# Another order for an encoder layer: transposes no longer kept in runs, shared transfer rates and two-way waits between VectorE and GpSimd in the MLP

## The chip, the cores and the metric

The kernel runs on one core of a Trainium2 chip. The time is the device time of one execution in microseconds (us); it was 708.28 us in the median of three runs. The engines of a core are TensorE (PE, matrix products and transposes), VectorE (DVE), ScalarE (ACT), GpSimd (POOL) and SyncE (SP, which here only issues transfers). PEld is the loading of weights into PE. Each engine takes its instructions in the order in which the program lists them, and waits on semaphores for the others.

## The reference

One layer (SEQ 512, D_MODEL 1024, D_FF 2816): a combined input projection feeds three groups of attention heads (A differential, B with forget gates, C over chunks), then an output projection, a gated MLP with a causal convolution of width 3, and a gated embedding.

```python
def reference(x, p, ln_mix, w_in, ...):
    h = x
    for i in range(DEPTH):
        hn = rms_norm(h, ln_mix[i])
        z = hn @ w_in[i]
        (q1, q2, k1, k2, va, qf, kf, vf, fg, qc, kc, vc) = jnp.split(z, IN_SPLITS, axis=-1)
        ...
        o_a = diff_attention(q1, q2, k1, k2, va, lam, subln_gain[i], lam_init)
        o_b = forgetting_attention(qf, kf, vf, log_f)
        o_c = chunk_attention(qc, kc, vc, rel_bias[i])
        h = h + jnp.concatenate([o_a, o_b, o_c], axis=-1) @ w_out[i]
        h = h + conv_gated_mlp(rms_norm(h, ln_ffn[i]), w_up[i], conv_w[i], conv_b[i], w_down[i])
        gate = jax.nn.sigmoid(rms_norm(h, ln_ple[i]) @ w_ple_gate[i])
        h = h + (p[i] @ w_ple_proj[i]) * gate
    return h

def conv_gated_mlp(h, w_up, conv_w, conv_b, w_down):
    u = h @ w_up
    ...
    gate, val = jnp.split(c, 2, axis=-1)
    return (jax.nn.silu(gate) * val) @ w_down
```

## The kernel before

All large products are made three times in a reduced format: an operand is cast to a high part (`whi`, `Th`, made by ACT) and the remainder is a low part (`wlo`, `Tl`, a DVE subtraction), and PE adds high·high, high·low and low·high into one PSUM bank. So each block of weights, 128 by 768 numbers, costs a transfer into `wraw` (SP queue), a cast, a subtraction, and then PE's products. Scores are `s<-k,q`, probabilities are `e`, transposed by PE against `ident` into banks `t`, and multiplied with `V` into `o`. `z`, `s`, `t` and `o` are the PSUM banks (2, 2, 3 and 1 of them). The sums for the queries' and keys' norms end in POOL powers (`rs<-rs,nhalf`) and POOL scalings (`k<-k`, `q<-q`).

In the MLP some of the products are made from sums of weight blocks, by a scheme that saves products (`up_seven`, `down`). POOL forms the sums (`wraw<-wraw,wraw`), or a transfer on POOL's own queue adds one block onto another on its way in; names with `again` are tiles used a second time.

Nothing of this is issued when the Python code runs through it. Each instruction is recorded in a `Plan` with a price; there is one plan for attention (from the first products to the output projection), another for the MLP and the rest. `Plan.due` gives each PE instruction a due time, the sum of the PE work recorded before it plus a number for its group from the table `SHIFT`; other engines' instructions are due before their readers. `Plan.solve` then walks forward in time: of the instructions that are free on an engine it takes the one due first. `Plan.emit` issues them in that order, and the order on each engine is pinned. Because of that every recorded instruction has the line of the one helper that issues it: L357 before (in `Engine.now`), L391 after the change.

Four rules of `solve` and `emit` belong to the change:

- Transfers: one wire for both queues, served in turn, at a rate of 0.37 MB per us for SP and 0.105 for POOL, with 2.0 us ahead and 0.6 behind.
- Runs of transposes: when PE has just made a transpose, another one that is free is preferred to a matmul (and the other way round) if it is due no more than `STICK` = 2.0 us later; a matmul after a lone transpose is priced 0.08 us higher.
- PE prefers instructions whose inputs have been ready for `SURE` = 0.1 us.
- Waits without data ("port"): in the second plan (`late` is 0.1 there and 0 in the first) a POOL instruction of over 0.6 us that follows a DVE instruction with all its inputs in SBUF is made to wait for it. `Engine.behind` adds such a wait.

Of the kernel before, what the change touches and what calls it, by code (L numbers as in the profile page):

```python
# [41 lines left out]
for _i in range(3):  # L42
# [5 lines left out]
AHEAD = 2  # L48
# [75 lines left out]
class Plan:  # L124
# [5 lines left out]
    def __init__(self, clock, there=(), mem=None, fresh=0.0, late=0.0):  # L130
        self.group, self.loaded, self.fresh, self.late = "first", set(), fresh, late
        self.clock, self.there, self.ops, self.mem = clock, [(v.tensor.name, self.region(v), t) for v, t in there], [], mem or {}

    @staticmethod
    def region(v):
        size = 2 if v.dtype == BF16 else 4
        (row, pn), *rest = [tuple(x) for x in v.ap]
        if v.tensor.space == bass.MemoryType.DRAM and v.tensor.name not in STAND_INS:
# [45 lines left out]
    def price(self, op):  # L184
# [4 lines left out]
        op.move, op.turns = 0, op.name == "transpose"  # L189
# [29 lines left out]
    LONG, STICK = 0.6, 2.0  # L219
    HW, SW, AT_ONCE = 0.37e6, 0.105e6, 8  # L220
    SURE, AHEAD, MUCH, WAIT = 0.1, 1.0, 2.0, 0.6
# [3 lines left out]
    def due(self, shift):  # L225
# [5 lines left out]
        for op in reversed(self.ops):  # L231
            if op.eng.name != "pe":
                spent = op.busy + op.lag + 0.05 + (op.move / self.HW + 2.0 if op.move else 0.0)
                op.dl = min([q.dl for q in op.next], default=t) - spent

    def solve(self):
# [6 lines left out]
        wire, out, order = 0.0, {"sp": [], "pool": []}, []  # L243
        turns, alone = False, False
        held = {"dve": 0.0, "pool": 0.0}
        other = {"dve": "pool", "pool": "dve"}
        when = lambda q: max(q.at, held[other[q.eng.name]] + (self.late if q.eng.name == "pool" else 0.0)) if q.port else q.at
        rank = lambda q: (q.dl, q.pos)
        while True:
            best = None  # L250
            for e in self.ENGINES:
                if free[e]:
                    t = max(clock[e], min(when(q) for q in free[e]))
                    if best is None or t < best[0]:
                        best = t, e
            if best is None:
# [3 lines left out]
            if e == "pe":  # L260
                can = [q for q in can if q.at + self.SURE <= t] or can
            op = min(can, key=rank)
            if e == "pe" and op.turns != turns:
                same = [q for q in can if q.turns == turns and q.dl < op.dl + self.STICK]
                if same and (turns or sum(q.turns and q.dl < op.dl + self.STICK for q in can) < 2 or min(q.dl for q in same) < op.dl + self.STICK / 2):
                    op = min(same, key=rank)
# [12 lines left out]
            if e == "pe":  # L279
                busy += 0.08 * (alone and not op.turns)  # L280
                turns, alone = op.turns, op.turns and not turns
            if op.move:
                done = out[e]
                if len(done) >= self.AT_ONCE:
                    t0 = max(t0, done[-self.AT_ONCE])
                wire = max(t0 + 2.0, wire) + op.move / (self.HW if e == "sp" else self.SW)
                op.end = wire + 0.6
                done.append(op.end)
# [7 lines left out]
            for q in op.next:  # L296
                q.left -= 1
                q.at = max(q.at, op.start if e == "pe" and q.eng is op.eng else op.end + self.LEAD[q.eng.name])
                if not q.left:
                    free[q.eng.name].append(q)  # L300
# [4 lines left out]
    def emit(self):  # L305
# [3 lines left out]
        before = None  # L309
        for op in self.choose():  # L310
            op.ins = op.eng.now(op.name, [real(v) for v in op.a], {q: real(v) for q, v in op.k.items()})
            if op.port:
                if before and op.eng.name == "pool" and before.eng.name == "dve" and op.busy > self.LONG and self.late:
# [1744 lines left out]
```

## Time and profile before

| | us |
|---|---|
| runs | 709.49, 708.25, 708.28 (median 708.28) |
| profiled execution, its own time | 707.89 |
| its span (first to last instruction) | 706.0 |
| granted clock of TensorE in it, mean | 0.998 |

| engine | busy us | share of the span |
|---|---|---|
| PE | 690.3 | 98% |
| DVE | 552.5 | 78% |
| ACT | 408.7 | 58% |
| POOL | 300.6 | 43% |

The costliest groups of instructions, by line, engine, operation, names and tile, then count, busy us, mean ns of one, and the engine's idle time before them with what ended it:

```profile
L357 ACT CAST whi<-wraw 128x768 fp32r<-128x768 f32 (+2 forms) x140 | 106.1, 768 | 59.9 <-POOL wraw L357 11.4
L357 PE MATMUL z<-whi,Th 128*128 128x384 f32 (+2 forms) x356 | 123.4, 351 | 4.5 <-ACT whi L357 4.5
L357 DVE TENSOR_TENSOR wlo<-wraw,whi 128x768 fp32r<-128x768 f32 (+2 forms) x122 | 111.5, 930 | 15.4 <-ACT whi L357 13.6
L357 POOL TENSOR_TENSOR wraw<-wraw,wraw 128x256 f32<-128x256 f32 (+1 forms) x22 | 28.3, 1285 | 101.3 <-DVE wlo L357 53.6
```

The mean duration of a matmul is longer than its spacing, since the next one starts before the last one's end: 128x512 matmuls follow each other at 0.233 us, 384 columns at 0.174, 256 at 0.118, transposes at 0.109. Where the text speaks of a loss, it is the distance from start to start less this spacing. A DVE, ACT or POOL instruction that is idle on its own account says nothing; what counts is whether PE waits.

### The profile page before, as it was taken

The page shows a single profiled execution, that of the slowest core. Times are in us where ns is not written, and L with a number is a line of the kernel's source. Part 1 is how long each engine was busy: PE and PEld are TensorE (multiplying, and loading weights), DVE is VectorE, ACT ScalarE, POOL GpSimd, SP SyncE. Part 2 cuts the span into 40 slices and gives each one's busy share as a digit, 9 for nine tenths or more (in the row PEclk, how much of TensorE's full clock was granted, in tenths as well). Part 3 has the DMA queues.
Part 4 walks back from the last instruction along what each step waited for, and adds up shares of the span by engine and source line. Part 5 has one row for each costly group of instructions (what it writes and reads, how often), then busy time and mean ns, then how long its engine had stood idle before and what let it go on. Part 6 is the DMA issues. An engine that isn't in the chain of part 4 may idle for free.

```text
span 706.0 us, 12402 instructions
## 1 busy us (share of the span) xinstructions
PE 690.3 (98%) x4420; PEld 636.4 (90%) x4420; DVE 552.5 (78%) x1126; ACT 408.7 (58%) x781; POOL 300.6 (43%) x403
## 2 busy tenths in 40 slices
PE   7999999999999999999999999999999999999997
PEld 7999999898999888899998999889988888999886
DVE  7679878879788666789888887997877998878722
ACT  6657676565766575666666435665345674536711
POOL 3788677766665452223223334304432203245200
PEclk9999999999999999999999999999999999999999
DMA  9523444423112252584763278651488552204521
GB/s 321 201 83 111 125 117 128 118 60 109 45 61 76 75 124 83 200 244 105 214 159 113 68 186 207 163 162 33 139 211 209 183 168 82 91 32 155 163 85 46
DMA packets 41275, 92.72 MB, mean 131 GB/s; under 512 B 4694, under 2 KB 7510, under 8 KB 41212
## 3 DMA queue, kind: packets, MB, share of 16 engines
q1 hardware_dynamic: 34572, 78.24, 33.1%
q0 software_dynamic: 6352, 13.38, 10.8%
q8 instruction: 35, 0.57, 0.3%
q10 hardware_dynamic: 288, 0.30, 0.1%
q14 instruction: 28, 0.23, 0.1%
HBM read 83.63 MB, written 4.21 MB: 124 GB/s over the span
## 4 chain that ended last, share of the span: by engine, by line
PE 91%; DVE 3%; DMA 2%; ACT 2%; POOL 1%; issue 1%; ACTq 0%; POOLq 0%
PE z L357 46%; PE s L357 22%; PE t L357 16%; PE o L357 7%; DMA wraw<-in_w_up_dram 1%; DVE wlo L357 1%; POOL k L357 1%; POOL q L357 1%; ACT whi L357 1%; DMA zn<-in_w_in_dram 0%; DVE e L357 0%; DVE conv L357 0%; POOL rs L357 0%; ACT e L357 0%; DVE kl L357 0%
## 5 line engine op out<-in xcount | busy, mean ns | idle before, releaser
L357 ACT CAST whi<-wraw 128x768 fp32r<-128x768 f32 (+2 forms) x140 | 106.1, 768 | 59.9 <-POOL wraw L357 11.4
L357 PE MATMUL z<-whi,Th 128*128 128x384 f32 (+2 forms) x356 | 123.4, 351 | 4.5 <-ACT whi L357 4.5
L357 DVE TENSOR_TENSOR wlo<-wraw,whi 128x768 fp32r<-128x768 f32 (+2 forms) x122 | 111.5, 930 | 15.4 <-ACT whi L357 13.6
L357 PE MATMUL z<-wlo,Th 128*128 128x384 f32 (+2 forms) x356 | 123.0, 350 | 0.0
L357 PE MATMUL z<-whi,Tl 128*128 128x384 f32 (+2 forms) x356 | 121.8, 347 | 0.0
L357 PEld LDWEIGHTS z<-whi,Th 128*128 128x128 f32 x356 | 66.9, 189 | 8.0 <-ACT whi L357 4.5
L357 POOL TENSOR_TENSOR wraw<-wraw,wraw 128x256 f32<-128x256 f32 (+1 forms) x22 | 28.3, 1285 | 101.3 <-DVE wlo L357 53.6
L357 PEld LDWEIGHTS z<-wlo,Th 128*128 128x128 f32 x356 | 67.2, 189 | 4.0 <-DVE wlo L357 0.4
L357 PEld LDWEIGHTS z<-whi,Tl 128*128 128x128 f32 x356 | 67.0, 189 | 3.8
L357 ACT ACTIVATE e<-e,st 128x128 f32<-128x128 f32 (+3 forms) x80 | 44.7, 560 | 29.8 <-DVE st L357 29.4
L357 PE MATMUL z<-Th,whi 128*128 128x512 f32 (+1 forms) x156 | 53.2, 346 | 1.4 <-ACT whi L357 1.3
L357 PE MATMUL s<-Th,whi 128*128 128x512 f32 (+1 forms) x156 | 53.3, 345 | 0.6 <-ACT whi L357 0.6
L357 PE MATMUL s<-Th,wlo 128*128 128x512 f32 (+1 forms) x156 | 53.7, 345 | 0.0
L357 PE MATMUL s<-Tl,whi 128*128 128x512 f32 (+1 forms) x156 | 53.6, 345 | 0.0
L357 PE MATMUL z<-Tl,whi 128*128 128x512 f32 (+1 forms) x156 | 53.5, 344 | 0.0
L357 PE MATMUL z<-Th,wlo 128*128 128x512 f32 (+1 forms) x156 | 53.4, 344 | 0.0
L357 POOL TENSOR_TENSOR rs<-rs,nhalf 128x4 f32<-128x4 f32 x40 | 43.5, 1091 | 4.8 <-DVE rs L357 2.3
L357 DVE CUSTOM_DVE_ANT_0 e<-s,bias 128x128 f32<-128x128 f32 (+3 forms) x74 | 33.7, 469 | 12.4 <-PE s L357 7.2
L357 DVE TENSOR_TENSOR conv<-conv,conv 128x512 f32<-128x512 f32 (+1 forms) x31 | 21.0, 691 | 24.0 <-ACT conv L357 23.8
L357 POOL TENSOR_SCALAR e<-e,st 128x512 f32<-128x512 f32 (+3 forms) x48 | 27.2, 576 | 18.1 <-DVE st L357 16.8
L357 PEld LDWEIGHTS z<-Th,whi 128*128 128x128 f32 x156 | 29.1, 188 | 4.8 <-ACT whi L357 1.8
L357 PEld LDWEIGHTS s<-Th,whi 128*128 128x128 f32 x156 | 29.2, 188 | 3.8 <-ACT whi L357 0.8
(352 smaller groups left out, 2152.4 us busy)
## 6 DMA issues: line engine op xcount, KB each, us to landing
wraw<-in_w_up_dram SPq DMA_DIRECT2D x41, 384.0 KB, 4.3
wraw<-in_w_in_dram SPq DMA_DIRECT2D x28, 384.0 KB, 3.7
wraw<-in_w_down_dram SPq DMA_DIRECT2D x16, 384.0 KB, 3.6
whi_again<-in_w_up_dram SPq DMA_DIRECT2D x11, 384.0 KB, 4.5
wraw<-in_w_out_dram SPq DMA_DIRECT2D x16, 256.0 KB, 2.7
wlo_again<-in_w_up_dram SPq DMA_DIRECT2D x10, 384.0 KB, 4.3
wraw<-in_w_up_dram SPq DMA_DIRECT2D x15, 256.0 KB, 4.1
wlo<-wraw POOLq DMA_DIRECT2D x7, 384.0 KB, 4.2
```

What stands on the lines that cost most here:

```text
L357: ins = getattr(self.eng, op)(*a, **k)
```

## The change

The `SHIFT` table gets other numbers for all of its groups. The runs of transposes are no longer kept and the 0.08 us for a lone transpose go. `SURE` becomes an argument: 0.15 us in the first plan, and in the second the fifth argument, 0.1, that was `late`, is now `sure`. In the second plan each queue has its own transfers in flight, at rates that depend on whether the other queue moves data too; the first plan (`apart=True`) has both queues at their single rates, independent of each other. The waits without data are set both ways: an instruction of over 0.25 us of either engine waits for the other engine's last one if it is planned to start less than `NEAR` after that one's end; in the first plan none is set, as before. The last line of `region` tells the planner which parts of the output two stores touch.

```diff
@@ Plan.__init__ @@
-    def __init__(self, clock, there=(), mem=None, fresh=0.0, late=0.0):
+    def __init__(self, clock, there=(), mem=None, fresh=0.0, sure=0.15, apart=False):
+        self.sure, self.apart = sure, apart
+        if apart:
+            one = {"sp": 0.37e6, "pool": 0.105e6}
+            self.RATE, self.SENT, self.ARRIVED = {k: {e: one[e] for e in k} for k in self.RATE}, {"sp": 2.0, "pool": 2.0}, 0.6
+            self.HANDED = {"pool": 0.0, "dve": 0.0}
@@ SHIFT @@
-    "first": -11.4, "in1_0": -0.3, "in1_1": -25, "in1_2": -2.7, "A0a": -6.5, "in1_3": -12.1, "in2_0": -5.9,
...
@@ constants @@
-    LONG, STICK = 0.6, 2.0
-    HW, SW, AT_ONCE = 0.37e6, 0.105e6, 8
-    SURE, AHEAD, MUCH, WAIT = 0.1, 1.0, 2.0, 0.6
+    SHORT, HANDED, NEAR = 0.25, {"pool": 0.2, "dve": 0.1}, {"pool": 1.0, "dve": 0.6}
+    RATE = {("sp",): {"sp": 0.334e6}, ("pool",): {"pool": 0.164e6}, ("sp", "pool"): {"sp": 0.143e6, "pool": 0.078e6}}
+    SENT, ARRIVED, AT_ONCE = {"sp": 1.46, "pool": 1.49}, 0.58, 8
+    AHEAD, MUCH, WAIT = 1.0, 2.0, 0.6
@@ solve @@
-        when = lambda q: max(q.at, held[other[q.eng.name]] + (self.late if q.eng.name == "pool" else 0.0)) if q.port else q.at
+        def when(q):
+            if q.port:
+                return max(q.at, held[other[q.eng.name]] + self.HANDED[q.eng.name])
+            if q.move:
+                return max(q.at, gate[q.eng.name]) if len(wire[q.eng.name]) < self.AT_ONCE else never
+            return q.at
+        def landed(until):
...
+                busy = tuple(e for e in wire if wire[e] and wire[e][0][1] <= now)
+                rate = self.RATE.get(busy, {})
...
-                can = [q for q in can if q.at + self.SURE <= t] or can
+                can = [q for q in can if q.at + self.sure <= t] or can
             op = min(can, key=rank)
-            if e == "pe" and op.turns != turns:
-                same = [q for q in can if q.turns == turns and q.dl < op.dl + self.STICK]
-                if same and (turns or sum(q.turns and q.dl < op.dl + self.STICK for q in can) < 2 or min(q.dl for q in same) < op.dl + self.STICK / 2):
-                    op = min(same, key=rank)
...
-                busy += 0.08 * (alone and not op.turns)
...
-                wire = max(t0 + 2.0, wire) + op.move / (self.HW if e == "sp" else self.SW)
-                op.end = wire + 0.6
+                wire[e].append([op, t0 + self.SENT[e], op.move])
@@ emit @@
-                if before and op.eng.name == "pool" and before.eng.name == "dve" and op.busy > self.LONG and self.late:
-                    op.eng.behind(op.ins, before.ins)
-                before = op
+                e = op.eng.name
+                d = last["pool" if e == "dve" else "dve"]
+                if d and not self.apart and d is not known[e] and op.busy > self.SHORT and op.start < d.start + d.busy + self.NEAR[e]:
+                    op.eng.behind(op.ins, d.ins)
+                    known[e] = d
+                last[e] = op
@@ the attention plan @@
-    PLAN.append(Plan({"act": 2.95, "dve": 0.9, "pool": 3.9, "sp": 0.73, "pe": 1.0}, ((WA[0], 3.85), (cols, 4.6), (ident, 2.6))))
+    PLAN.append(Plan({"act": 2.95, "dve": 0.9, "pool": 3.9, "sp": 0.73, "pe": 1.0}, ((WA[0], 3.85), (cols, 4.6), (ident, 2.6)), apart=True))
```

Both programs have the same instructions. Three places show how the order moves. The first is GpSimd at the scores of pair B0 (at about 119 to 124 us of the profile before). `rs` are the norms' factors, `q` and `k` the scaled queries and keys, and `k_154<-k_154` is the last scaling ahead of the score `s_131<-k_154,q_151`. Before:

```order
L357 TENSOR_SCALAR rs_139<-rs_139,rstd 128x4
L357 TENSOR_TENSOR rs_139<-rs_139,nhalf 128x4
L357 TENSOR_SCALAR q_152<-q_151 64x512
L357 TENSOR_SCALAR rs_140<-rs_140,rstd 128x4
L357 TENSOR_SCALAR k_155<-k_154 64x512
L357 TENSOR_TENSOR rs_140<-rs_140,nhalf 128x4
L357 TENSOR_SCALAR k_155<-k_154 64x512
L357 TENSOR_SCALAR q_151<-ql_153 64x512
L357 TENSOR_SCALAR k_154<-k_154 64x512
```

and after the change:

```order
L391 TENSOR_SCALAR e_0_133<-e_0_133,st_166,nlam_145 128x256
L391 TENSOR_SCALAR e_0_143<-e_0_143,st_163,nlam_145 128x128
L391 TENSOR_SCALAR e_1_94<-e_1_94,st_168,nlam_145 128x384
L391 TENSOR_SCALAR q_152<-q_151 64x512
L391 TENSOR_SCALAR e_1_96<-e_1_96,st_170,nlam_145 128x512
L391 TENSOR_SCALAR k_155<-k_154 64x512 x2
L391 TENSOR_SCALAR q_151<-ql_153 64x512
L391 TENSOR_SCALAR k_154<-k_154 64x512
L391 TENSOR_SCALAR rs_139<-rs_139,rstd 128x4
```

The powers of `rs_139` and `rs_140` have moved behind the scaling of `k_154`, and a scaling of probabilities (`e_1_96`) stands closer ahead of it.

The second place is TensorE at pair B1's score (at about 157 to 160 us): `o_148` are products of probabilities with `V`, `s_130` is the score, and `z_129` a product of the input projection. Before:

```order
L357 MATMUL t_146<-ident,e_1_94 128x128
L357 MATMUL t_146<-ident,e_1_96 128x128
L357 MATMUL t_146<-ident,e_0_143 128x128
L357 MATMUL z_129<-whi_117,Th_64 128x384
L357 MATMUL o_148<-pth_174,V_183 128x512
L357 MATMUL s_130<-k_160,q_158 128x512
```

and after:

```order
L391 MATMUL t_149<-ident,e_1_161 128x128
L391 MATMUL z_129<-wlo_111,Th_64 128x384
L391 MATMUL z_129<-whi_110,Tl_66 128x384
L391 MATMUL o_148<-pth_174,V_183 128x512
L391 MATMUL o_148<-ptl_175,V_183 128x512
L391 MATMUL o_148<-pth_181,V_183 128x384
L391 MATMUL o_148<-ptl_182,V_183 128x384
L391 MATMUL o_148<-ptc_0_137,V_183 128x256
L391 MATMUL s_130<-k_160,q_158 128x512
```

Five products into `o_148` now stand between the pieces ahead and the score, where one stood. Among the transposes (`t<-ident,e`) single ones now stand between matmuls.

The third place is VectorE in the MLP, at about 500 us, with what each instruction waits for (the number behind an engine's name is the program's own for a semaphore). `wlo_113` is the low part of a weight block loaded a second time; `h` are the sums into the residual. Before:

```order
L357 TENSOR_TENSOR h<-h,t_146 128x2x256 [waits PE_49]
L357 TENSOR_TENSOR h<-h,o_148 128x2x256
L357 TENSOR_TENSOR h<-h,t_150 128x2x256 [waits PE_49]
L357 TENSOR_TENSOR wlo_113<-wlo_again,whi_112 128x768 [waits Activation_49]
L357 TENSOR_TENSOR wlo_115<-wraw_116,whi_114 128x768 [waits DMAHW4_49]
```

and after:

```order
L391 SCALAR_TENSOR_TENSOR conv_3069<-s_130,cols,conv_3069 128x510 [waits DVE_49]
L391 TENSOR_TENSOR h<-h,t_150 128x2x256 [waits PE_49]
L391 TENSOR_TENSOR h<-h,o_148 128x2x256 [waits PE_49]
L391 TENSOR_TENSOR wlo_113<-wlo_again,whi_112 128x768 [waits Activation_49,Pool_49]
L391 TENSOR_TENSOR wlo_118<-wraw_119,whi_117 128x768 [waits DMAHW6_49,Activation_49]
```

The subtraction into `wlo_113` waits for GpSimd too. On GpSimd, the instruction that it waits for, a sum into `wraw_122`, itself follows a transfer of its own queue:

```order
L391 TENSOR_TENSOR whi_again<-wraw_125,wraw_119 128x768 [waits Activation_49]
L391 DMA wraw_122<-in_w_up_dram 128x256 [waits DMAHW5_49]
L391 TENSOR_TENSOR wlo_again<-wlo_again,whi_again 128x768 [waits DVE_49,DMAHW3_49,Activation_49,Pool_49]
L391 TENSOR_TENSOR wraw_122<-wraw_122 128x256 [waits DMASW0_49]
L391 DMA wraw_125<-in_w_up_dram 128x768 [waits DMAHW0_49]
```

That sum of 128x256 waits for the transfer two rows above it (`DMASW0_49`); before the change both stood further on, behind the loads of `whi_again` and `wraw_125`.

More of the change, by code (lines that the diff above doesn't have):

```diff
@@ L128 @@
     LEAD = {"act": 0.035, "dve": 0.035, "pool": 0.095, "pe": 0.055, "sp": 0.1}
-    def __init__(self, clock, there=(), mem=None, fresh=0.0, late=0.0):
-        self.group, self.loaded, self.fresh, self.late = "first", set(), fresh, late
+    def __init__(self, clock, there=(), mem=None, fresh=0.0, sure=0.15, apart=False):
[4 more added lines that the diff above has]
+            self.HANDED = {"pool": 0.0, "dve": 0.0}
+        self.group, self.loaded, self.fresh = "first", set(), fresh
         self.clock, self.there, self.ops, self.mem = clock, [(v.tensor.name, self.region(v), t) for v, t in there], [], mem or {}
@@ L137, in region @@
         (row, pn), *rest = [tuple(x) for x in v.ap]
-        if v.tensor.space == bass.MemoryType.DRAM and v.tensor.name not in STAND_INS:
+        if v.tensor.space == bass.MemoryType.DRAM and v.tensor.name not in STAND_INS and v.tensor.name != "out_dram":
             return 0, 1, v.offset * size, (v.offset + (pn - 1) * row + sum((n - 1) * st for st, n in rest) + 1) * size
@@ L188, in price @@
         acc = "accum_out" in k
-        op.move, op.turns = 0, op.name == "transpose"
+        op.move = 0
         if e == "pe":
@@ L232, in due @@
             if op.eng.name != "pe":
-                spent = op.busy + op.lag + 0.05 + (op.move / self.HW + 2.0 if op.move else 0.0)
+                spent = op.busy + op.lag + 0.05 + (op.move / 0.37e6 + 2.0 if op.move else 0.0)
                 op.dl = min([q.dl for q in op.next], default=t) - spent
@@ L242, in solve, with release @@
                 free[op.eng.name].append(op)
-        wire, out, order = 0.0, {"sp": [], "pool": []}, []
-        turns, alone = False, False
+        wire, now, gate, order = {"sp": [], "pool": []}, 0.0, {"sp": 0.0, "pool": 0.0}, []
         held = {"dve": 0.0, "pool": 0.0}
         other = {"dve": "pool", "pool": "dve"}
-        when = lambda q: max(q.at, held[other[q.eng.name]] + (self.late if q.eng.name == "pool" else 0.0)) if q.port else q.at
+        never = 1e18
+        def when(q):
[4 more added lines that the diff above has]
+            return q.at
+        def release(op, e):
+            for q in op.next:
+                q.left -= 1
+                q.at = max(q.at, op.start if e == "pe" and q.eng is op.eng else op.end + self.LEAD[q.eng.name])
+                if not q.left:
+                    free[q.eng.name].append(q)
+        def landed(until):
+            nonlocal now
+            while now < until:
+                busy = tuple(e for e in wire if wire[e] and wire[e][0][1] <= now)
+                rate = self.RATE.get(busy, {})
+                step, who = until - now, None
+                for e in wire:
+                    if e in rate and wire[e][0][2] / rate[e] <= step:
+                        step, who = wire[e][0][2] / rate[e], e
+                    if wire[e] and e not in rate and wire[e][0][1] - now < step:
+                        step, who = wire[e][0][1] - now, None
+                now = until if step == until - now else now + step
+                for e in rate:
+                    wire[e][0][2] -= rate[e] * step
+                if who:
+                    op = wire[who].pop(0)[0]
+                    op.end = now + self.ARRIVED
+                    if len(wire[who]) + 1 >= self.AT_ONCE:
+                        gate[who] = op.end
+                    return op, who
+            return None
         rank = lambda q: (q.dl, q.pos)
@@ L255, in solve @@
                         best = t, e
+            there = landed(best[0] if best else never) if wire["sp"] or wire["pool"] else None
+            if there:
+                release(*there)
+                continue
             if best is None:
@@ L278, in solve @@
             busy = op.busy * (1.85 if e == "pe" and t0 < 8.6 else 1.0)
-            if e == "pe":
-                busy += 0.08 * (alone and not op.turns)
-                turns, alone = op.turns, op.turns and not turns
             if op.move:
-                done = out[e]
-                if len(done) >= self.AT_ONCE:
-                    t0 = max(t0, done[-self.AT_ONCE])
-                wire = max(t0 + 2.0, wire) + op.move / (self.HW if e == "sp" else self.SW)
-                op.end = wire + 0.6
-                done.append(op.end)
+                wire[e].append([op, t0 + self.SENT[e], op.move])
             else:
@@ L295, in solve @@
             order.append(op)
[L296 to L300, printed above, removed]
+            if not op.move:
+                release(op, e)
         assert len(order) == len(self.ops)
@@ L308, in emit @@
                 d.next.append(op)
-        before = None
+        last, known = {"dve": None, "pool": None}, {"dve": None, "pool": None}
         for op in self.choose():
```

75 rows, old and new, of the table SHIFT are left out of this document.

## The prediction

> **What bounds the kernel now.** I read the page's totals first, then the chain that ended last, then what TensorE (PE) waited for, then the busy time by stretches.
>
> ```profile
> span 706.0 us, 12402 instructions
> PE 690.3 (98%) x4420; PEld 636.4 (90%) x4420; DVE 552.5 (78%) x1126; ACT 408.7 (58%) x781; POOL 300.6 (43%) x403
> ...
> PE 91%; DVE 3%; DMA 2%; ACT 2%; POOL 1%; issue 1%; ACTq 0%; POOLq 0%
> ...
> PE z L357 <- ACT whi L357: 5.8, 2, 4.5
> PE s L357 <- POOL k L357: 2.1, 3, 1.3
> PE s L357 <- DVE st L357: 1.3, 2, 1.1
> PE s L357 <- ACT whi L357: 0.6, 1, 0.6
> ...
> 700.48 0.28 PE L357 MATMUL z<-ah_real,Tl 128*128 128x256 f32 x1
> ```
>
> PE is busy for 690.3 of 706.0 us and is 91% of the chain. So the kernel is a queue of matmuls, and an order can only save what PE idles: 706.0 − 690.3 = 15.7 us. Two pieces of that are out of the order's reach. The first wait for the cast whi is 4.5 us long: it is the wait before the first matmul. The last matmul starts at 700.48 and lasts 0.28, so 5.24 us follow it (sigmoid, product, sum, the last store); the change leaves that tail's steps as they are. Some 5.9 us inside the program remain. The stretches (length, then busy time of PE, PEld, DVE, ACT, POOL, clock, DMA share, GB/s) say where:
>
> ```profile
> 0.00:20.00 20.00, 15.52 (x89) 15.53 (x90) 14.89 (x31) 13.32 (x25) 6.19 (x15) 1.00 0.92 332
> 20.00:60.00 40.00, 39.42 (x261) 37.98 (x260) 29.81 (x90) 24.75 (x60) 33.20 (x53) 1.00 0.33 114
> 60.00:120.00 60.00, 59.76 (x389) 57.36 (x388) 51.58 (x144) 42.69 (x103) 43.94 (x62) 1.00 0.49 133
> 120.00:170.00 50.00, 46.86 (x285) 43.58 (x284) 41.33 (x137) 32.00 (x78) 33.40 (x47) 1.00 0.35 101
> 170.00:260.00 90.00, 90.00 (x529) 83.36 (x528) 68.30 (x196) 55.48 (x137) 53.32 (x85) 1.00 0.25 71
> 500.00:520.00 20.00, 18.68 (x151) 18.16 (x150) 14.22 (x20) 7.88 (x12) 7.22 (x6) 1.00 0.69 187
> 520.00:560.00 40.00, 39.43 (x243) 34.96 (x242) 32.44 (x52) 23.42 (x37) 13.80 (x18) 1.00 0.68 183
> ```
>
> PE idles 0.58 us in 20 to 60, 0.24 in 60 to 120, 3.14 in 120 to 170, nothing from 170 to 260, then 1.32 and 0.57 between 500 and 560. The granted clock is 1.00 in all of them. Attention (to about 260) has some 4 us to give, the MLP some 2. Everything below is about these 6 us, and about what a new order can add where PE now waits for nothing.
>
> **The change part by part.** Both programs hold the same instructions; their order on each engine differs, and so do waits between VectorE (DVE) and GpSimd (POOL) that no datum asks for.
>
> *The start.* The new order runs all of the first unit's products before the next unit's join in, and the SP queue loads the x and weight rows for them first, the next unit's weights and the x rows of the residual later. In the first 20 us PE idles 20 − 15.52 = 4.48, which is the wait before the first matmul and nothing else, so nothing is to be had there: **0**, ends −0.3 and +0.6 (a late weight at the handover would cost what the small wait for whi costs, 0.6).
>
> *Pair B0's first score, at 124 us.* The planner prices transposes and matmuls freely now, and the pieces around this score trade places.
>
> ```profile
> 122.77 0.38 PE L357 MATMUL t<-ident,zn 128*128 128x128 f32 x2
> 124.41 0.39 PE L357 MATMUL s<-k,q 128*128 128x256 f32 x1 [1.26 <-POOL k L357]
> ...
> 119.98 1.02 POOL L357 TENSOR_TENSOR rs<-rs,nhalf 128x4 f32<-128x4 f32 x1
> 121.09 0.62 POOL L357 TENSOR_SCALAR k<-k 64x512 fp32r<-64x512 f32 x1
> 121.78 1.99 POOL L357 TENSOR_SCALAR q<-ql 64x512 fp32r<-64x512 f32 x1
> ...
> L357 POOL TENSOR_SCALAR e<-e,st 128x512 f32<-128x512 f32 (+3 forms) x48 | 27.2, 576 | 18.1 <-DVE st L357 16.8
> ```
>
> PE's two transposes (0.109 each, from the spacing in the transpose rows below) end their turn at 122.99, and the score starts at 124.41: 1.42 us lost. It waits for the last k scaling, which stands on POOL behind the power rs (1.02) and a q that took 1.99 where the k ahead of it, of the same shape, took 0.62. In the new order the powers rs stand behind this k, and one e scaling stands closer ahead of it. PE work between the release of the chain and the score goes from 6.33 to 6.49 us (the order's matmuls, each at its spacing), so almost all of the gain must come from POOL: 1.02 less, some 0.4 to 0.6 more for the e (0.576 in the mean of its forms), so 0.4 to 0.6 at the least; at most the whole 1.42, if q also keeps clear of DVE. I take **−1.0**, between the ends. If it isn't so, the score is late by the same 1.4.
>
> *Pair B1's score, at 159 us.*
>
> ```profile
> 157.83 0.40 PE L357 MATMUL o<-pth,V 128*128 128x512 f32 x1
> 159.28 0.50 PE L357 MATMUL s<-k,q 128*128 128x512 f32 x1 [1.06 <-DVE st L357]
> ...
> 155.95 3.01 DVE L357 TENSOR_TENSOR wlo<-wraw,whi 128x768 fp32r<-128x768 f32 x1
> 155.98 2.15 POOL L357 TENSOR_TENSOR wlo<-wraw,whi 128x768 fp32r<-128x768 f32 x1
> 158.88 0.34 DVE L357 CUSTOM_DVE_ANT_0 e<-s,fbias,st 128x128 f32<-128x128 f32 x1
> ...
> L357 DVE TENSOR_TENSOR wlo<-whi_again,whi 128x768 fp32r<-128x768 f32 x18 | 17.2, 954 | 3.1 <-ACT whi L357 3.0
> ```
>
> One 128x512 matmul takes 0.233 from start to start, so the score could start at 158.06; it loses 1.22. DVE's subtraction took 3.01 us where the same form takes 0.954 in the MLP: POOL's own subtraction (2.15) ran over it, and DVE ended 0.83 after POOL. The row e queued behind it frees the score's bank. In the new order five products o stand ahead of this score instead of one, and more behind; PE's work since the release rises from 1.18 to 3.60 us, 2.4 more against 1.22 lost. I take **−1.2**; the least is 0, if two such subtractions meet again at another place.
>
> The Trainium skill (SBUF — State Buffer, section "Who interferes with whom") says that VectorE and GpSimd share one pair of ports as an exclusive lock, whoever issues first holding it for the whole instruction, and that a VectorE operation with both inputs in SBUF contends with GpSimd's reads. The two rows agree (3.01 is close to 2.15 + 0.954), and the rule speaks against the MLP part of the change: there a written wait would only repeat what the ports do, saving nothing, so that the sum keeps zero for these waits and only their cost can appear.
>
> *The other attention waits.* By the stretches they are 0.58 + 0.24 + (3.14 − 1.42 − 1.22 = 0.50) = 1.32 us. Of the nine places behind them five get a good deal more PE work between release and use in the new order (29.46: 4.3 to 10.4 us; 135.25: 5.0 to 9.7; 129.91: 3.7 to 11.6), three a few tenths, one loses 1.6. I take two thirds, **−0.9**; the ends are 0 and −1.3.
>
> *Broken runs of transposes.* The 312 transposes stand in 137 runs instead of 67, 73 of them single.
>
> ```profile
> 37.38 0.34 PE L357 MATMUL z<-whi,Th 128*128 128x384 f32 x1
> 37.55 0.49 PE L357 MATMUL t<-ident,zn 128*128 128x128 f32 x3
> 37.80 0.42 PE L357 MATMUL z<-wlo,Th 128*128 128x384 f32 x1
> 38.06 0.33 PE L357 MATMUL z<-whi,Tl 128*128 128x384 f32 x1
> ```
>
> From 37.38 to 38.06 are 0.68 us for two matmuls of 384 columns (0.174 each between neighbours) and three transposes (0.109 each): 0.675. A change of kind costs about 0.005, so 70 more runs are **+0.3**, with ends 0 and 0.7.
>
> *New tight places.* I count as many chains with under 0.5 us of slack after as before (149 to 150); two are newly tight, both scores in attention. The row of waits for POOL k gives 2.1/3 = 0.7 each; at even odds two of them are **+0.7**, ends 0 and 2.8 (two like 1.42).
>
> *The MLP's late weights.* Rates shared by the two DMA queues change when loads are issued.
>
> ```profile
> 515.51 0.50 PE L357 MATMUL z<-Th,whi 128*128 128x512 f32 x1 [1.32 <-ACT whi L357]
> 514.62 0.83 ACT L357 CAST whi<-wlo_again 128x768 fp32r<-128x768 f32 x1 [7.21 <-DVE h L357]
> 507.88 0.33 SPq L357 DMA_DIRECT2D wlo_again<-in_w_up_dram  x1
> ...
> wlo_again<-in_w_up_dram SPq DMA_DIRECT2D x10, 384.0 KB, 4.3
> 545.09 0.50 PE L357 MATMUL s<-Th,whi 128*128 128x512 f32 x1 [0.57 <-ACT whi L357]
> ```
>
> The cast at 514.62 waits for a load issued at 507.88, some 6.7 us where the median is 4.3. After the change the same chain (accumulated load, POOL sum, DVE subtraction, reload, cast, matmul) has 0.1 to 0.2 us of slack at the median, so with the slow transfer it is late again: **0**, ends −1.3 (it lands on time) and +2.4 (as slow as here once more, 6.7 − 4.3). The wait at 545 goes in most ways in which the loads can be reordered: **−0.4** of 0.57.
>
> *DVE behind POOL.* Waits without a datum behind them: POOL had 49 for DVE and has 40; DVE had none for POOL and has 36, all in the MLP. Queued behind each on DVE are h sums, which free PE's banks, and weight subtractions, which PE waits for. I take **0**: from 260 to 650 DVE idles
>
> ```profile
> 260.00:650.00 390.00, 322.27 (x495) 1.00 0.50 144
> ```
>
> 67.7 us, 0.14 per instruction, and a hold at the ports exists already without a wait. If that cover is gone the price is the second rival's.
>
> The profiled execution took 707.89 us. In the order of the parts, 707.89 + 0 − 1.0 − 1.2 − 0.9 + 0.3 + 0.7 + 0 − 0.4 + 0 = 705.4; the median of the runs, 708.28, lies 0.4 above, so **705.8 us**.
>
> **The rivals.** *No net change, 708.2 us.* As many tight places as before means that new waits take the place of the old: all gains of 3.5 are eaten. For it speaks the equal count; against it that the two largest waits had named causes which the new order moves apart.
>
> *Slower, 711.5 us: a DVE instruction waits behind a POOL sum that waits for a transfer.*
>
> ```profile
> POOL wraw L357 <- DMA wraw<-in_w_up_dram: 19.5, 7, 7.7
> POOL whi_again L357 <- DMA whi_again<-in_w_up_dram: 9.8, 2, 6.3
> POOL wlo_again L357 <- DMA wlo_again<-in_w_up_dram: 4.2, 2, 3.5
> ```
>
> POOL stands waiting for a transfer 11 times, 33.5 us, 3.05 each. Thirteen of the 36 new waits name a POOL sum that follows an accumulated load. DVE's order is fixed, so each h sum and subtraction behind it is late by the same amount, and PE's three t banks fill. With 0.3 us of cover each hit is about 2.75; two hits of the thirteen are 5.5, and 705.8 + 5.5 is 711.3, some 711.5 with a tight weight. It decides as soon as such a transfer lands later than planned by more than DVE's slack there. Against it: DVE's idle 67.7 us, and that the planner prices transfers in a queue more slowly when both queues run. That late-MLP chains of a load and a sum with under 1 us of slack go from none to two or three speaks for it.
>
> *More gained, 702.5 us.* All visible idle goes: 1.42 + 1.22 + 1.32 in attention, 1.32 + 0.57 in the MLP, 5.85 less than 708.28. Against it: every former wait must vanish and none appear.
>
> **How the numbers follow.** Forecast 0.50, slower rival 0.30, no net change 0.10, more gained 0.10. The forecast's own range is 703 to 708: its low end has −1.4 at 124, −1.3 for the small waits and −1.3 at 515; its high end leaves the two large waits half in place and pays 2.8 for new ones. Faster or slower by 0.2% (1.4 us, what a measurement of this kernel can tell from none) means below 706.9 or above 709.7. Some eight tenths of the forecast and all of the last case are faster: 0.51. The rest of the forecast and most of the second are the same: 0.17. Slower is 0.32, nearly all from its rival. The range 701.5 to 712.0 takes in the last case's value and the slower rival's at two hits, and leaves out three hits.
>
> **What would show it.** In attention: no idle above 0.5 us before the B0 and B1 scores, PE busy over 48.5 of the 50 us around 120 to 170, and transposes at 0.109 spacing singly too. In the MLP: PE idle near the z product of the reloaded weight as before, and DVE rows "waiting for POOL" that PE doesn't follow. I am wrong if PE waits for DVE's h or wlo in the MLP for more than 2 us in all, if single transposes cost over 0.02 more each (70 of them 1.4), or if the B0 score keeps its wait with POOL's powers moved.

## The result, and the profile after

The change made the kernel slower: 710.55 us in the median (708.59 to 713.82, 15 runs) against 708.25 of the kernel before on the same chips (706.51 to 710.59, 15 runs), a ratio of 1.0036 with a 95% interval of 1.0026 to 1.0046. A second measurement, among the experiments, gave 1.0064 (1.0039 to 1.0088). 0.1% is 0.7 us.

The page of the changed kernel, its totals and the chain that ended last:

```profile
span 710.2 us, 12417 instructions
PE 694.4 (98%) x4420; PEld 637.2 (90%) x4420; DVE 546.7 (77%) x1126; ACT 409.0 (58%) x781; POOL 289.8 (41%) x403
...
PE 78%; DMA 11%; DVE 5%; ACT 2%; issue 2%; POOL 1%; SPq 0%; POOLq 0%; ACTq 0%; DVEq 0%
```

The chain is no longer PE's alone. It runs 11% through transfers, where it was 2%. The stretches of the changed kernel (length, then busy PE, PEld, DVE, ACT, POOL, clock, DMA share, GB/s):

```profile
20.00:60.00 40.00, 39.52 (x267) 37.96 (x266) 30.91 (x88) 25.17 (x60) 30.11 (x48) 1.00 0.37 112
60.00:120.00 60.00, 59.98 (x396) 57.38 (x395) 53.71 (x156) 41.98 (x103) 42.91 (x63) 1.00 0.50 133
120.00:170.00 50.00, 49.74 (x301) 46.93 (x300) 40.99 (x134) 33.74 (x81) 32.47 (x49) 1.00 0.32 85
260.00:400.00 140.00, 137.53 (x865) 122.10 (x864) 106.71 (x167) 79.94 (x128) 32.37 (x48) 1.00 0.52 149
400.00:500.00 100.00, 98.70 (x684) 90.71 (x684) 77.74 (x117) 53.11 (x80) 34.14 (x31) 1.00 0.53 147
500.00:520.00 20.00, 20.00 (x171) 20.00 (x170) 16.61 (x23) 5.50 (x8) 5.76 (x6) 1.00 0.59 140
520.00:560.00 40.00, 37.56 (x229) 33.03 (x229) 32.40 (x51) 23.43 (x38) 11.23 (x15) 1.00 0.76 203
```

and the two stretches of the kernel before that the prediction didn't show:

```profile
260.00:400.00 140.00, 140.00 (x895) 125.81 (x895) 115.69 (x192) 88.61 (x147) 38.41 (x56) 1.00 0.50 149
400.00:500.00 100.00, 99.91 (x705) 93.10 (x704) 83.62 (x123) 51.80 (x79) 34.83 (x31) 1.00 0.55 147
```

From 120 to 170 us PE now idles 0.26 us where it idled 3.14: attention gave what it had. From 260 to 560 it idles 2.47 + 1.30 + 0 + 2.44 = 6.21 us where it idled 0 + 0.09 + 1.32 + 0.57 = 1.98. What PE waited for, in all of the changed kernel:

```profile
PE z L391 <- ACT whi L391: 6.4, 3, 4.4
PE s L391 <- DVE conv L391: 1.0, 1, 1.0
PE s L391 <- ACT whi L391: 0.7, 1, 0.7
PE z L391 <- DVE wlo L391: 0.7, 1, 0.7
```

The waits of the scores for POOL's k and DVE's st are gone; those for cast weights are longer in sum, and those for DVE's `wlo` and `conv` are new. From 260 to 560 us PE now waits ten times, 0.27 to 1.04 us each, where it waited twice (1.32 at 515.51 and 0.57 at 545.09). The longest of the ten, followed backward through the timelines of PE, ACT, SP, DVE and POOL:

```profile
521.49 0.51 PE L391 MATMUL z<-Th,whi 128*128 128x512 f32 x1 [1.04 <-ACT whi L391]
...
520.61 0.83 ACT L391 CAST whi<-wlo_again 128x768 fp32r<-128x768 f32 x1 [1.63 <-DMA wlo_again<-in_w_up_dram]
...
514.89 0.33 SPq L391 DMA_DIRECT2D wlo_again<-in_w_up_dram  x1
...
513.90 0.96 DVE L391 TENSOR_TENSOR wlo<-wlo_again,whi 128x768 fp32r<-128x768 f32 x1 [2.08 <-POOL wraw L391]
...
513.13 0.73 POOL L391 TENSOR_TENSOR wraw<-wraw 128x256 f32<-128x256 f32 x1 [1.80 <-DMA wraw<-in_w_up_dram]
```

The POOL sum stands 1.80 us until its added transfer has landed; the DVE subtraction stands 2.08 us behind the sum, though it needs nothing of it; the reload into the tile that the subtraction has read is issued at 514.89 and its cast starts at 520.61; PE idles 1.04. That is the mechanism and the chain of the prediction's slower rival. But it is no new loss: it is the matmul that waited 1.32 us at 515.51 in the kernel before, for the same weight. The wait of 0.57 at 545.09 is there again too, with 0.98 at 544.47. New are the other eight, 4.2 us together. One of them, followed back through PE, ACT and POOL:

```profile
435.16 0.39 PE L391 MATMUL s<-xh,whi 128*128 128x256 f32 x1 [0.69 <-ACT whi L391]
...
434.28 0.83 ACT L391 CAST whi<-whi_again 128x768 fp32r<-128x768 f32 x1
...
433.15 1.05 POOL L391 TENSOR_TENSOR whi_again<-whi_again,wlo_again 128x256 f32<-128x256 f32 x1
...
431.19 0.86 POOL L391 DMA_DIRECT2D wraw<-in_w_up_dram  x1 [5.58 <-DMA wraw<-in_w_up_dram]
```

Here POOL stands 5.58 us until a load into `wraw` has landed, its sums come late behind that, then the casts, then PE. POOL's waits for transfers in the whole MLP have doubled, from 33.5 us to 64.9:

```profile
POOL wraw L391 <- DMA wraw<-in_w_up_dram: 43.3, 11, 9.8
POOL whi_again L391 <- DMA whi_again<-in_w_up_dram: 15.0, 3, 7.1
```

(the third, for `wlo_again`, is 6.6 us).

### The profile page after: what moved, and what is told of

Its sections match the earlier page's. It is cut to its first block, busy times and chain, and to the rows that moved or that the text cites. A ratio compares the mean times of both kernels' runs of the same rounds, so it can differ in the third digit from the quotient of the medians.

```text
span 710.2 us, 12417 instructions
## 1 busy us (share of the span) xinstructions
PE 694.4 (98%) x4420; PEld 637.2 (90%) x4420; DVE 546.7 (77%) x1126; ACT 409.0 (58%) x781; POOL 289.8 (41%) x403
## 3 DMA queue, kind: packets, MB, share of 16 engines
HBM read 83.63 MB, written 4.21 MB: 124 GB/s over the span
## 4 chain that ended last, share of the span: by engine, by line
PE 78%; DMA 11%; DVE 5%; ACT 2%; issue 2%; POOL 1%; SPq 0%; POOLq 0%; ACTq 0%; DVEq 0%
PE z L391 43%; PE s L391 16%; PE t L391 13%; PE o L391 6%; DMA wraw<-in_w_up_dram 5%; DVE wlo L391 3%; DMA whi_again<-in_w_up_dram 2%; ACT whi L391 1%; DVE conv L391 1%; DMA h<-in_x_dram 1%; DMA e<-in_w_in_dram 1%; DMA wraw<-in_w_in_dram 1%; DMA zn<-in_w_in_dram 1%; DMA whi_again<-in_w_down_dram 1%; SPq L391 0%
## 5 line engine op out<-in xcount | busy, mean ns | idle before, releaser
L391 DVE TENSOR_TENSOR wlo<-wraw,whi 128x768 fp32r<-128x768 f32 (+2 forms) x122 | 105.8, 882 | 21.9 <-ACT whi L391 16.5
L391 POOL DMA_DIRECT2D wraw<-in_w_up_dram x18 | 16.1, 949 | 54.0 <-DMA wraw<-in_w_up_dram 36.3
L391 POOL TENSOR_SCALAR e<-e,st 128x256 f32<-128x256 f32 (+3 forms) x48 | 29.2, 643 | 10.2 <-DVE st L391 8.3
```

The costliest lines, as they stand in the source:

```text
L391: ins = getattr(self.eng, op)(*a, **k)
```

## The experiments

The ratios are against the kernel before on the same chip, five rounds each. Wherever possible the order on each engine was kept row by row, so that only one thing differs. "Idle" in the tables is PE's idle time from 260 to 560 us by the stretches of the profile; it counts from the modelled end of the last matmul, so that a wait costs somewhat more from start to start (0.46 against 0.30 us for the one at 378.18 in the changed kernel).

### Each half alone

Both planners stand in one program. The half that is not changed gets the order and the waits of the other kernel row for row, since the MLP is planned from the end times that its own planner gives its own attention.

```diff
-    PLAN.append(Plan({"act": 2.95, "dve": 0.9, ...}, ..., apart=True))
+    PLAN.append(NewPlan({"act": 2.95, "dve": 0.9, ...}, ..., apart=True))   # OldPlan in the second kernel
-    PLAN.append(Plan(first.last, (), first.mem, first.last["dve"] + 0.6, 0.1))
+    PLAN.append(OldPlan(first.last, (), first.mem, first.last["dve"] + 0.6, 0.1))   # NewPlan in the second
```

> Attention in the order of the change, MLP instruction for instruction in the order and with the waits of before. In the two profiles the stalls of TensorE between 20 and 270 us fell from 8.1 to 4.7 us, those behind 270 us rose from 2.8 to 9.8. If the attention half is a gain of its own (both theories): 2 to 3.4 us under the kernel before, 705 to 706.5 us. If the gain is noise of one profile: within 1 us of 708.3.

> Attention as before, MLP in the order and with the waits of the change. Both theories: the loss is all here, 4 to 7 us over the kernel before, 712 to 715 us. If the halves do not add up (the change at +2.5 us is not the sum of this and of the attention half), the handover between them matters.

| | median us | ratio | idle |
|---|---|---|---|
| new attention, old MLP | 705.92 | 0.9958 (0.9944 to 0.9971) | 1.81 |
| old attention, new MLP | 715.19 | 1.0096 (1.0080 to 1.0112) | 6.11 |

The change is two changes of opposite sign: attention gains 3.0 us (2.1 to 4.0), the MLP loses 6.8 (5.7 to 7.9). The sum, 3.8, lies between the two measurements of the change, 2.5 and 4.5. The first of these kernels is faster than both the kernel before and the changed one.

### The waits between VectorE and GpSimd

The changed kernel in its own order, first without VectorE's waits, then without any that no datum asks for; the third is the kernel before without GpSimd's.

```diff
-                if d and not self.apart and d is not known[e] and ...
+                if e == "pool" and d and not self.apart and d is not known[e] and ...   # first
+                if False and d and not self.apart and d is not known[e] and ...         # second
-                if before and ... and op.busy > self.LONG and self.late:
+                if before and ... and op.busy > self.LONG and self.late and False:      # third
```

> The changed kernel, the same order on every engine, without the 36 waits of VectorE behind GpSimd. Theory W (the second rival of the prediction: VectorE stands behind sums that wait for a transfer): most of the MLP's 7 us of stalls goes, 704 to 707 us, and VectorE no longer stands 2.08 us before the subtraction at 513.9 us. Theory T (the order issues the reloads too late, whatever VectorE waits for): within 1.5 us of the changed kernel, 709 to 711.5 us, with the same late casts of whi.

> The changed kernel in the same order without any wait between VectorE and GpSimd that no datum asks for, neither the 36 of VectorE nor the 40 of GpSimd. Theory W: as the kernel without VectorE's waits, 704 to 707 us, up to 1 us more if GpSimd's sums now run over VectorE's subtractions and stretch them. Theory T: 709 to 711.5 us.

> The kernel before, the same order on every engine, without GpSimd's waits behind VectorE in the MLP. In the changed order these waits were worth 17 us. If they are worth that because an unpriced GpSimd sum takes the ports from a VectorE subtraction that TensorE waits for, it holds in this order too: 715 to 728 us. If it hung on the changed order: within 3 us of 708.3.

| | median us | ratio | idle |
|---|---|---|---|
| change without VectorE's waits | 709.22 | 1.0004 (0.9988 to 1.0020) | 4.38 |
| change without any | 726.08 | 1.0252 (1.0232 to 1.0271) | 13.90 |
| before without GpSimd's | 737.73 | 1.0415 (1.0394 to 1.0436) | 11.98 |

VectorE's 36 waits cost 0.3 to 0.6% (1.0036 and 1.0064 against 1.0004; the runs are of different sets), 2 to 4 us. That is part of the MLP's loss, not all of it: 3.3 us remain against the kernel with the new attention alone. The time, 709.22, lies in theory T's range at its low end and not in theory W's, but each has a part of the loss. In this kernel the subtraction of the chain at 521 us starts without a wait for POOL, and the 1.04 us on PE are gone, as are the waits at 353.68, 420.34 and 435.16 (2.75 us with it; others grow, so that the idle time falls by 1.8):

```profile
510.27 1.15 DVE L391 TENSOR_TENSOR wlo<-wlo_again,whi 128x768 fp32r<-128x768 f32 x1 [0.42 <-ACT whi L391]
```

GpSimd's waits are another matter: without them the changed order loses 16.9 us more and the order of before 30, both more than either expectation allowed. The timelines of POOL and DVE in the changed kernel without any waits, at 378 us:

```profile
377.98 2.18 POOL L391 TENSOR_TENSOR whi_again<-wlo_again,whi_again 128x768 f32<-128x768 f32 x1 [10.20 <-DVE wlo L391]
...
378.37 2.61 DVE L391 TENSOR_TENSOR wlo<-wraw,whi 128x768 fp32r<-128x768 f32 x1
```

The sum goes first, where in the changed kernel it starts behind the subtraction, and the subtraction takes 2.61 us instead of 0.95. PE waits for the steps behind it and loses 2.34 us at this place (from start to start, less the spacing), where the changed kernel loses 0.46. In the order of before the subtractions of 128x768 behind 260 us are longer too, 1.15 to 1.34 us in the mean of each form where they were 0.95 to 1.00. So in both orders an early POOL sum is dear, and a wait that makes POOL stand back is worth it.

Not all of the 16.9 and 30 us is waiting. At the end of PE's longest waits the profile grants half the clock for a while. In the changed order without any waits, PE's waits of 1.83, 2.18 and 2.07 us end at 344.81, 382.90 and 413.53 us, and the stretches there are:

```profile
345.20:348.60 3.40, 3.40 (x16) 3.37 (x16) 1.84 (x4) 1.34 (x2) 0.00 (x0) 0.51 0.40 124
382.80:386.20 3.40, 3.30 (x11) 2.94 (x12) 1.36 (x2) 0.63 (x1) 1.97 (x2) 0.50 0.00 0
413.50:416.90 3.40, 3.37 (x16) 3.37 (x17) 1.35 (x2) 0.82 (x2) 1.06 (x1) 0.50 0.00 0
```

In the order of before the clock is halved for 20.4 us (from 502.6, 547.0, 628.9 and 666.5 us), 17.25 of them busy. Half of the busy time at half clock is an estimated 5 of the 16.9 us and 9 of the 30. In the kernel before and in the changed one the clock is 1.00 in all stretches from 260 to 560 us. That the long waits bring the lower clock about is likely by these times, not tested.

### The transfers

The planner's dates can be set against the trace. For each transfer of 256 KB or more between 260 and 560 us, the table has the mean difference of its landing from the planned one, less TensorE's own lag behind its plan at that time, and the planned and true duration from issue to landing.

| queue, kernel | transfers | lands late by, mean us | over 1 us late | planned, true us |
|---|---|---|---|---|
| SP, before | 96 | −0.99 | 1 | 4.91, 4.36 |
| SP, change | 97 | 0.01 | 25 | 4.21, 4.41 |
| POOL, before | 18 | −1.32 | 2 | 6.48, 5.68 |
| POOL, change | 18 | 0.75 | 10 | 6.16, 6.31 |

The old prices were too long, and everything behind a load had about 1 us to spare. The new ones are nearer to the mean and have no room for the spread. The true durations of SP's loads hardly differ; what moved is the plan. (An expectation below names 14 late loads of 67 against 4 before, by a narrower count; counted as in the table, the changed order without VectorE's waits has 20 of 97 on SP and 9 of 18 on POOL.) To see whether that makes the rest of the loss, transfers were shortened in the same order. In the first and the third kernel SP's MLP weight loads (after the first into each tile) bring half of their columns; in the second it is the transfers that POOL's queue adds onto weight blocks. The first two are without VectorE's waits, the third has them. The diff is that of the first and the third, shortened.

```diff
+            if op.move and op.eng.name == "sp" and not self.apart and k["in_"].tensor.name.startswith(("in_w_up", "in_w_down")):
+                ...
+                n = k["in_"].shape[1] // (2 if name in self.loaded else 1)
+                ...
+                k = {**k, "out": k["out"][:, :n], "in_": k["in_"][:, :n]}
```

> The changed kernel without VectorE's waits, same order on every engine; of the MLP's weight loads on the SP queue all but the first into each tile bring only the left half of their columns, so half of those weights is left from earlier blocks. Theory T, that loads which land later than planned make up what is left of the MLP's loss (in this order 14 of 67 large loads between 260 and 560 us landed over 1 us later than planned, where before it were 4): the MLP's stalls fall from 6.3 us to under 3, 704 to 706.5 us. If the order of the engines themselves is at fault: within 1 us of the kernel without VectorE's waits, 708 to 710 us.

> The changed kernel without VectorE's waits, the transfers that GpSimd's queue adds onto weight blocks in the MLP cut to half their columns (the sums are then wrong in the other half); SP's loads stay whole. If the two queues' sharing makes the loads late: most of what the halved SP loads gave, 704.5 to 706.5 us. If SP's own loads were priced too short: 707.5 to 709.5 us.

> The changed kernel with VectorE's 36 waits and its order, its MLP weight loads on the SP queue cut to the left half of their columns (but for the first into each tile), so half of those weights is left from earlier blocks. If the waits of VectorE cost because transfers are late (GpSimd's sums stand waiting, VectorE behind them): with loads early the waits cost nothing, and the time is within 0.8 us of the same kernel without them, 704 to 705.5 us. If the waits cost by themselves: some 2 us more, 706 to 708 us.

| | median us | ratio | idle |
|---|---|---|---|
| half SP loads, no VectorE waits | 704.63 | 0.9941 (0.9923 to 0.9958) | 1.69 |
| half added transfers, no VectorE waits | 704.46 | 0.9953 (0.9938 to 0.9968) | 2.02 |
| half SP loads, with VectorE's waits | 705.04 | 0.9959 (0.9944 to 0.9974) | 1.51 |

Either shortening takes away what was left of the loss. All three are as fast as new attention with the old MLP, and PE's idle time is back at that of before. Of the ten waits of PE two are left in the first and the third kernel. One of them, 0.96 us at 326.5 us, is in all three (the first load into each tile stays whole), so the shortening does not settle what causes that one. Whether shorter transfers would help the old order as well, whose largest wait in the kernel with the new attention is 1.42 us for a reloaded weight at 514.62, was not tried. With early loads VectorE's waits cost nothing that can be measured: 0.9959 against 0.9941 is 1.3 us, with an interval of −0.4 to 2.9, in sets on two chips. So they seem to be dear mainly where the POOL sum ahead of them stands waiting. POOL's waits for transfers in the MLP in the third kernel, 12.6 us where the changed one had 64.9:

```profile
POOL wraw L397 <- DMA wraw<-in_w_up_dram: 7.4, 4, 2.6
POOL wlo_again L397 <- DMA whi_again<-in_w_up_dram: 4.1, 1, 4.1
POOL whi_again L397 <- DMA whi_again<-in_w_up_dram: 1.1, 1, 1.1
```

The second kernel tells that the two queues act on each other: with less on POOL's queue, SP's loads, untouched, land 0.55 us before their planned date on the mean, where they land at it without VectorE's waits alone (0.02), and their mean time from issue to landing is 4.07 us instead of 4.45. How much of the gain is this, and how much the earlier sums behind the added transfers, was not separated.

### Rules and table

Three kernels ask which part of the MLP's plan is at fault, all with the new attention: the change with transfers planned to land 0.6 us later, the old rules with the new `SHIFT` table, the new rules with the old table.

```diff
+    PLAN[-1].ARRIVED = 1.18                                        # first
+    PLAN.append(OldPlan(first.last, ...)); rest.table = SHIFT_NEW   # second
+    PLAN.append(NewPlan(first.last, ...)); rest.table = SHIFT_OLD   # third
```

> The changed kernel, but the MLP's planner lets each transfer land 0.6 us later (0.58 becomes 1.18), so it leaves more room ahead of what reads them; the order of the MLP changes with it. Theory T: 707 to 709.5 us, fewer loads over 1 us late. If the margin of the transfers does not matter: within 1 us of the changed kernel or above it, 709.5 to 712 us.

> Attention as changed; the MLP planned by the rules of before (one wire at the old rates, runs of transposes, GpSimd alone waits) with the new table of numbers. If the rules are at fault: near the kernel with new attention and old MLP, 705 to 707.5 us. If the table is at fault: near the change or above it, 709.5 to 713 us.

> Attention as changed; the MLP planned by the new rules (shared rates, waits both ways) with the old table. If the rules are at fault: as slow as the change or slower, 710 to 714 us, with loads that land later than planned. If the table is at fault: 705 to 708 us.

They took 722.57 us (1.0206, 1.0179 to 1.0234), 715.43 us (1.0091, 1.0066 to 1.0117) and 725.26 us (1.0238, 1.0216 to 1.0260). All three are slower than the changed kernel, the second by the least (0.3 to 0.6%), and lie above every range that was expected, and they do not divide the loss. In the first, SP's loads do land early again (0.89 us before their planned dates on the mean, 2 of 95 over 1 us late, counted as above), and it is still 10 us and more slower than the change. So transfers that land by the plan are not enough when the order is another one. The likely reading is that a table of due times fits the prices under which it was made; in these three mixed cases the time is above either kernel's. It stays open whether the shorter prices alone made the loads late. Whether the new rates with more room and a table made for them would do better was not tried.

### The change once more

> The changed kernel itself, on the chip of the three kernels beside it, so that they can be compared. 709.5 to 712 us, 0.2 to 0.5% over the kernel before.

712.22 us, 1.0064 (1.0039 to 1.0088), just above the range expected. On the same chip the two kernels with half transfers took 704.46 and 705.04 us, 7.8 and 7.2 less.

## Why the prediction was wrong

**Attention: right, and a little small.** The terms −1.0, −1.2, −0.9, +0.3 and +0.7 sum to −2.1; the half alone gained 3.0 (2.1 to 4.0). The waits before the B0 and the B1 score are gone in whole, 1.42 and 1.22, and the new tight places (+0.7) did not show. The broken runs of transposes are no dearer than priced. Single ones on PE in the changed kernel:

```profile
72.80 0.27 PE L391 MATMUL t<-ident,e 128*128 128x128 f32 x1
72.82 0.37 PE L391 MATMUL z<-whi,Tl 128*128 128x256 f32 x1
73.03 0.28 PE L391 MATMUL t<-ident,e 128*128 128x128 f32 x1
73.06 0.37 PE L391 MATMUL z<-whi,Th 128*128 128x256 f32 x1
73.26 0.27 PE L391 MATMUL t<-ident,e 128*128 128x128 f32 x1
```

A transpose and a 256-column matmul follow each other in 0.23 us, and 0.109 + 0.118 is 0.227. The matmul starts 0.02 behind the transpose and the next instruction 0.21 behind the matmul, so the pair has to be read together.

**The MLP's late weights: the step that failed.** It was booked at 0 with ends of −1.3 and +2.4, and the wait at 545 at −0.4. It looked at the two places where PE waited already and took the rest as covered. At these two it came out nearly as booked: PE idles 1.04 and 0.98 us there, where it idled 1.32 and 0.57. The loss is at eight other matmuls, 4.2 us of idle time, for which the sum had no term. Without VectorE's waits about 3.3 us of the MLP's loss remain, and shorter transfers in the same order take them away, which puts them down to late transfers. The idle time from 260 to 500 us, 3.77 us where it was 0.09, is the sign of it. The prediction had what it took to suspect this: the diff prices a 384 KB load that runs alone at 1.46 + 0.393/0.334 + 0.58 = 3.22 us, where the old rule had 2.0 + 0.393/0.37 + 0.6 = 3.66, and the profile's median is 4.3. Cheaper prices put readers nearer to loads everywhere, not only where a wait shows. That the prices are the reason is argued from the table of landings; the run with longer prices changed the order too and did not show it.

**DVE behind POOL: booked at 0, cost 2 to 4 us.** DVE's idle 67.7 us was taken as cover, but a mean of 0.14 us per instruction says nothing of the place where POOL stands for a transfer. The slower rival named that place, the thirteen sums behind added transfers, and 711.3 us. It was right on the mechanism of this part, but it priced two hits at 5.5 us where the waits cost 2 to 4 and late loads, for which it had no term, the rest. That its time is near the measured one is partly luck: the MLP lost 6.8 us and attention gained 3.0, both more than it reckoned with. The prediction's own sign of being wrong, over 2 us of PE waiting for DVE's `h` or `wlo` in the MLP, came to 1.9 (0.7, 0.5, 0.4 and 0.3): the delays reached PE through casts and `conv` as well.

**The rule on the ports.** The prediction drew from it that a written wait repeats what the ports do, and that the MLP's waits can't gain. The runs show the other half: who goes first decides. GpSimd's waits, which make the sum stand back, are worth 17 to 30 us, the clock's part included; VectorE's, which make the subtraction stand back, cost. The prediction's two rows at 156 us do not show this: there DVE's record starts 0.03 us ahead of POOL's, and it is still DVE that is stretched. At 378 us POOL starts 0.39 us ahead. The Trainium skill (SBUF — State Buffer, section "Who interferes with whom") says as much, that issue order decides who blocks, and the rows at 378 us agree with it.

**The rivals of no net change and of more gained** both fell: the measured ratios leave 1 out, and the second's idle time went in attention alone.

## What to carry to other kernels

Where a planner's prices are made more exact, ask what margin the old errors held: here 1 of 96 SP loads priced 0.5 us too long was over 1 us late, and a quarter of those priced near the mean. A wait that was there before is no part of the loss, however clear its chain: compare the waits of both kernels matmul by matmul. Test the halves of a change apart before judging it, since a gain of 3 us stood behind a loss of 7. When two engines hinder each other, try letting the one whose result is not needed soon stand back, and do not queue an urgent instruction behind one that waits for a transfer.

## What had not been expected of the hardware

An early GpSimd sum is dearer than its length tells. Without the 49 waits of GpSimd behind VectorE the kernel before took 30 us more (737.73 against 707.78 us), though the sums that they hold back take 0.7 to 1.85 us each; an estimated 9 of the 30 are the halved clock. And the transfers of these two groups got longer in the median with the new order, at the same size, on SP's queue and on POOL's; the changed kernel's rows stand against 4.3 and 5.9 us before:

```profile
wraw<-in_w_up_dram SPq DMA_DIRECT2D x41, 384.0 KB, 4.8
...
wraw<-in_w_up_dram POOLq DMA_DIRECT2D x6, 384.0 KB, 7.0
```
